# An MLP whose second matmul uses seven products: all units fast, part of their factors made ahead, every sum carried by ScalarE

## The chip, the core and the metric

The kernel runs on one core of one Trainium2 chip. The metric is the device time of one execution in microseconds. The engines are named as in the profile: PE is TensorE, PEld its weight loads, DVE is VectorE, ACT is ScalarE, POOL is GpSimd and SP is SyncE, which here only issues transfers.

## What is computed

A decoder trunk of two layers over 256 positions and a model width of 2048, all in float32. Each layer is a mixer and an MLP with 8192 hidden columns, each followed by a layer norm of the residual.

```python
def sq_relu_mlp(x, w1, w2):
    return jnp.square(jax.nn.relu(x @ w1)) @ w2

def reference(x, ...):
    h = x
    for layer in range(2):
        if layer < 1:
            mix = short_conv_mixer(h, ...)      # (gate_b * conv(gate_c * u)) @ w_out
        else:
            mix = mla_mixer(h, ...)             # latent attention, 16 heads, then @ w_o
        h = layer_norm(ALPHA * h + mix, ln_g[layer, 0], ln_b[layer, 0])
        h = layer_norm(ALPHA * h + sq_relu_mlp(h, mlp_w1[layer], mlp_w2[layer]), ln_g[layer, 1], ln_b[layer, 1])
    return h
```

## The kernel before

**Numbers in two parts.** TensorE takes a rounded form of float32, so every operand is split into a rounded high part and the rest. `split` (L125 to L128) does this for weights: ScalarE casts the high part (L127), VectorE subtracts it to get the low part (L128). A product is then three terms: high by high, high by low, low by high.

**The stream of weights.** All weights pass once, in halves of 128 x 1024 (512 KB), in the order of the list `stream`. SyncE loads a half into one of five raw buffers (`RAW`), ScalarE and VectorE split it into one of eight high and low buffers (`WA`). `take` (L183) hands the next halves to TensorE's code and, first, issues the preparation of halves up to `LOOK` = 5 steps ahead. Each engine works through its instructions in the order in which they were issued, so this look-ahead decides how early a split stands in VectorE's order.

**The stages.** Layer 0's mixer is 48 products of 16 halves' rows each (`opening` for the first four, which are loaded in pieces of growing size, then `lagged`), the convolution, and the product with `w_out`. Layer 1's mixer is the attention and the product with `w_o`. Each MLP works through its hidden columns in eight parts, q = 0 to 7. In each part, eight products (`products`, L288, tile `ps_u`) give 1024 hidden columns, which are squared and split; then the second matmul adds their contribution to the 256 x 2048 result. Parts 0 and 7 do that plainly (`down`). Parts 1 to 6 (`FAST`) are called the fast stages here: they use units of seven products in place of eight (the Strassen-Winograd scheme on 2 x 2 blocks), in `down_pairs` (L634).

**A fast unit.** `prepare` (L141) loads two tiles r1 and r2, which hold the four blocks of the weight, and VectorE builds from them the sums of blocks that the scheme needs: `raw_t` (L162, 128 x 1024, the factors T1 and T3), T2 (L166) and T4 (L169), each 128 x 512. Four splits follow: r1, `raw_t`, r2 and T4 (tile `t`). `fast_products` (L343) then runs seven dots of three matmuls of 512 columns. The factors of the other side, `forms`, come from the hidden columns (`form`, L703).

**Groups and sums.** The 2048 result columns are two groups of 1024; each group has four units per stage. Group 1 is done first (tiles `ps_r`), then group 0 (`ps_f`). Of group 1's four units three are fast and the last is plain, two halves of eight dots (`MIXED = "sssp"`). Seven running sums per group are kept in SBUF, in `acc` and `sums`. At the start of a group ScalarE copies a sum into its PSUM bank (`resumed`, L612) so that the dots add onto it, and at the end copies it out (`put_back`, L616). Three sums of group 0 ("2", "6", "4") start from zero instead, and VectorE adds them (`keep`, L624). There are eight PSUM banks; while the eight products run, four of them (`busy`) take turns for `ps_u`.

Of the kernel before, what the change touches and what calls it, by code (L numbers as in the profile page):

```python
# [37 lines left out]
MIXED = "sssp"  # L38
EVEN = (QC - 1, "22")
# [7 lines left out]
WO_G = 3  # L47
BEHIND = (2, 2, 2, 3, 2, 2, 3)
# [5 lines left out]
def trunk(ctx: ExitStack, tc: tile.TileContext, xT, vecs, lead, w_first, w_in, w_out, w_kv, w_q, w_uk, w_uv,  # L54
# [22 lines left out]

    stream = []
# [4 lines left out]
    def mlp_stream(l):  # L83
        out = []
        for q in range(NQ):
            out += halves(w1[l, q * QC:(q + 1) * QC])
            if q not in FAST:
                out += halves(w2[l, q])
                continue
            for j, kind in enumerate(MIXED):  # L90
                out += [(w2f[l, q, 1, j, 0], w2f[l, q, 1, j, 1])] if kind == "s" else \
                    halves(w2[l, q, 2, j]) + halves(w2[l, q, 3, j])
            out += [(w2f[l, q, 0, j, 0], w2f[l, q, 0, j, 1]) for j in range(QC // 2)]
        return out
# [4 lines left out]
    stream += halves(w_o) + mlp_stream(1)  # L99

# [40 lines left out]
    def prepare(i):  # L141
# [7 lines left out]
        r1, r2 = (load_raw(f"{i}_{j}", src) for j, src in enumerate(stream[i]))  # L149
        out = []  # L150

        def finished(r, name):
# [3 lines left out]

        b22, (b21, b12) = r1[:, BW:], (r2[:, :BW], r2[:, BW:])
# [12 lines left out]
        f = state["fast"].tile([P, 2, BW], F32R, tag="t4", name=f"t4_{i}", bufs=2)  # L170
        split(f[:, 0, :], f[:, 1, :], t4)
        b1, t13, b2 = ([[v.rearrange("p b c -> p (b c)")[:, o:o + BW] for v in w] for o in (0, BW)] for w in out)
        ready[i] = {"11": b1[0], "22": b1[1], "21": b2[0], "T2": b2[1], "T1": t13[0], "T3": t13[1],
                    "T4": [f[:, 0, :], f[:, 1, :]]}
# [8 lines left out]
    def take(halves=2, look=LOOK):  # L183
# [3 lines left out]
        ahead = -sum(size(j) for j in range(i, i + halves))  # L187
        for j in range(i, len(stream)):
            for step in range(size(j)):
                ahead += 1  # L190
                if ahead > look:
                    return [ready.pop(i + k) for k in range(halves)]
# [6 lines left out]
        return [ready.pop(i + k) for k in range(halves)]  # L199
# [143 lines left out]
    def fast_products(ps, x, forms, j, fresh, ready, onto=()):  # L343
# [159 lines left out]
    def summed(ln, pss, add, m0=0):  # L503

        for m, ps in enumerate(pss, m0):
            add(ps, m)
# [40 lines left out]
    ln = Norm(0, ALPHA)  # L547
    for m in range(NC):
# [24 lines left out]
    summed(ln, chain(products(1, z), lagged(NC - 1, z)), residual)  # L573

    def mlp(idx, ln, blocks, fast, begin=None, extra=None, last=False):
# [32 lines left out]
        def resumed(p, g, name, bank):  # L608

            ps = psum(name, bank)  # L610
            if q != FAST[0] or p not in OWN:
# [3 lines left out]
        def put_back(p, g, ps):  # L615
            nc.scalar.copy(place(p, g), ps)  # L616

        def keep(p, g, ps):

            at = place(p, g)  # L620
            if q == FAST[0] and p in OWN:
# [4 lines left out]
        def resume(busy, free, ps, m):  # L626

            b2, b3, b4, b6 = free
            b1, b5, b7, b22 = busy
            for p, bank in {3: (("3", b3),), 4: (("2", b2),), 5: (("4", b4), ("1", b1)), 6: (("6", b6), ("5", b5)),  # L630
                            7: (("7", b7), ("22", b22))}.get(m, ()):
                ps[p] = resumed(p, 1, f"ps_r{p}", bank)

        def down_pairs(h, forms, busy, free, ps):  # L634

            b2, b3, b4, b6 = free
            b1, b5, b7, b22 = busy
            new = set(OWN) if q == FAST[0] else set()
            onto = set(ps) - new
            for j, kind in enumerate(MIXED):  # L640
                if kind == "s":
                    last = j == MIXED.rindex("s")
                    fast_products(ps, h, forms, j, new if j == 0 else (), OWN if last else (), onto)
                    if last:
                        for p in OWN:
                            put_back(p, 1, ps[p])
                        then = {p: resumed(p, 0, f"ps_f{p}", bank) for p, bank in (("3", b1), ("1", b5))}
                    continue
                for two in (((0, "2"), (1, "4")), ((1, "22"), (0, "3"))):
                    w, = take(1, LOOK + 1)  # L650
                    for t, p in two:
                        for kk in range(2):
                            k = 2 * j + kk
                            dot(ps[p], wide_rows(w, kk), held(h[k], t), False, k == QC - 1, (k, p) == EVEN, True)
                    if j == len(MIXED) - 1:
                        if "5" not in then:
                            then.update({p: resumed(p, 0, f"ps_f{p}", bank) for p, bank in (("5", b7), ("7", b6))})
                        for _, p in two:
                            put_back(p, 1, ps[p])
# [528 lines left out]
```

## Time and profile before

| | |
|---|---|
| median of three runs | 2000.02 us |
| lowest and highest run | 1996.99, 2000.58 us |
| span of the profiled execution, first to last instruction | 1994.9 us |
| TensorE clock granted, mean over the span | 1.000 |
| bytes moved, mean rate over the span | 385.85 MB, 193 GB/s |
| VectorE: splits of whole halves (L128, `lo`) | 710 of 1220 ns |
| ScalarE: casts of whole halves (L127, `hi`) | 710 of 1051 ns |

The span is one execution of its own; the runs were timed without the profiler, so the two stand side by side and neither is derived from the other. A row of a group gives the line, the engine, the operation, output and input with their shapes, the count, the busy time, the mean time of one in ns, and the idle time in front of these instructions with what ended most of it. The mean of one instruction contains its latency; instructions of one engine follow each other at a shorter pitch, which the start times in the timeline give.

### The profile page before, as it was taken

How to read it: one execution, taken by the hardware profiler on the slowest of the kernel's cores; microseconds unless marked ns; L12 is line 12 of the kernel's file. 1: busy time of each engine (PE TensorE's matmuls, PEld its weight loads, DVE VectorE, ACT ScalarE, POOL GpSimd, SP SyncE). 2: the span in 40 equal slices, each digit the busy share in tenths (PEclk: the TensorE clock that was granted, in tenths of full speed). 3: DMA queues.
4: the chain of work that ended last, by engine and by line, in shares of the span. 5: the costliest groups of instructions: out<-in, count | busy, mean ns of one | idle time of the engine just before them, and what ended most of it. 6: DMA issues, size and time to landing. Idle time of an engine off the chain costs nothing.

```text
span 1994.9 us, 30180 instructions
## 1 busy us (share of the span) xinstructions
PE 1987.7 (100%) x11110; PEld 1737.2 (87%) x11110; DVE 1709.4 (86%) x2555; ACT 1354.9 (68%) x2154; POOL 2.3 (0%) x21
## 2 busy tenths in 40 slices
PE   9999999999999999999999999999999999999998
PEld 8888888988888888888889998898888888888886
DVE  8667667797999989989978988777899999999985
ACT  6444445586778778777756755558677787887772
POOL 0000000000000000000000000000000000000000
PEclk9999999999999999999999999999999999999999
DMA  8666666565657466574855543656464656656483
GB/s 318 205 191 187 190 190 190 179 193 157 212 170 251 148 216 221 177 243 147 281 171 159 170 140 123 201 180 195 146 233 155 232 161 220 222 178 233 150 269 130
DMA packets 106853, 385.85 MB, mean 193 GB/s; under 512 B 11857, under 2 KB 12625, under 8 KB 106449
## 3 DMA queue, kind: packets, MB, share of 16 engines
q1 hardware_dynamic: 106560, 383.79, 59.5%
q8 instruction: 87, 1.43, 0.3%
q14 instruction: 62, 0.50, 0.1%
q10 hardware_dynamic: 144, 0.13, 0.0%
HBM read 381.78 MB, written 2.10 MB: 192 GB/s over the span
## 4 chain that ended last, share of the span: by engine, by line
PE 98%; DVE 1%; ACT 1%; issue 0%; DVEq 0%; ACTq 0%
PE ps_u L215 20%; PE ps_l L215 13%; PE ps_u L219 10%; PE ps_l L219 7%; PE ps_f L300 4%; PE ps_f L303 4%; PE ps_f L302 4%; PE ps_r L303 4%; PE ps_r L302 4%; PE ps_r L300 4%; PE ps_d L300 2%; PE ps_d L302 2%; PE ps_d L303 2%; PE ps_w L249 2%; PE ps_w L248 2%; PE ps_w L247 2%
## 5 line engine op out<-in xcount | busy, mean ns | idle before, releaser
L128 DVE TENSOR_TENSOR lo<-raw,hi 128x1024 fp32r<-128x1024 f32 x710 | 861.8, 1220 | 190.6 <-ACT hi L127 119.9
L127 ACT CAST hi<-raw 128x1024 fp32r<-128x1024 f32 x710 | 741.8, 1051 | 247.4 <-PE ps_l L215 98.1
L215 PE MATMUL ps_u<-xhl,hi 128*128 128x512 f32 x1792 | 621.7, 392 | 0.0
L219 PE MATMUL ps_u<-xhl,lo 128*128 128x256 f32 x1792 | 498.2, 279 | 0.0
L215 PEld LDWEIGHTS ps_u<-xhl,hi 128*128 128x128 f32 x1792 | 334.5, 187 | 73.6 <-ACT acc L595 0.2
L219 PEld LDWEIGHTS ps_u<-xhl,lo 128*128 128x128 f32 x1792 | 338.1, 189 | 1.8
L215 PE MATMUL ps_l<-xhl_a,hi 128*128 128x512 f32 x704 | 244.1, 393 | 0.0
L219 PE MATMUL ps_l<-xhl_a,lo 128*128 128x256 f32 x704 | 195.4, 279 | 0.0
L215 PEld LDWEIGHTS ps_l<-xhl_a,hi 128*128 128x128 f32 x704 | 132.1, 188 | 29.9
L219 PEld LDWEIGHTS ps_l<-xhl_a,lo 128*128 128x128 f32 x704 | 131.9, 188 | 0.2
L127 ACT CAST hi_t<-raw_t 128x1024 fp32r<-128x1024 f32 x84 | 88.5, 1054 | 45.8 <-DVE raw_t L162 41.4
L162 DVE TENSOR_TENSOR raw_t<-raw,raw 128x1024 f32<-128x1024 f32 x84 | 102.3, 1218 | 1.8 <-DMA raw<-in_w2f_dram 1.5
L128 DVE TENSOR_TENSOR lo_t<-raw_t,hi_t 128x1024 fp32r<-128x1024 f32 x84 | 102.4, 1219 | 0.2
L718 ACT ACTIVATE fp<-fp 128x256 f32<-128x256 f32 x96 | 40.0, 416 | 63.2 <-DVE fp L356 62.6
L215 PE MATMUL ps_l<-z,hi 128*128 128x512 f32 x240 | 82.4, 391 | 0.0
L300 PE MATMUL ps_d<-hi,h 128*128 128x512 f32 x192 | 75.0, 391 | 0.0
L302 PE MATMUL ps_d<-lo,h 128*128 128x512 f32 x192 | 75.0, 390 | 0.0
L303 PE MATMUL ps_d<-hi,h 128*128 128x512 f32 x192 | 74.8, 389 | 0.0
L249 PE MATMUL ps_w<-xd,hi 128*128 128x258 f32 x256 | 72.7, 284 | 0.0
L248 PE MATMUL ps_w<-xd,lo 128*128 128x258 f32 x256 | 72.3, 282 | 0.0
L247 PE MATMUL ps_w<-xd,hi 128*128 128x258 f32 x256 | 72.3, 282 | 0.0
L215 PE MATMUL ps_l<-oT,hi 128*128 128x512 f32 x208 | 71.3, 391 | 0.0
(296 smaller groups left out, 3963.7 us busy)
## 6 DMA issues: line engine op xcount, KB each, us to landing
raw<-in_w_dram SPq DMA_DIRECT2D x344, 512.0 KB, 4.5
raw<-in_w2f_dram SPq DMA_DIRECT2D x168, 512.0 KB, 3.9
raw<-in_w_in_dram SPq DMA_DIRECT2D x88, 512.0 KB, 4.2
raw<-in_w_out_dram SPq DMA_DIRECT2D x32, 512.0 KB, 3.7
raw<-in_w_o_dram SPq DMA_DIRECT2D x32, 512.0 KB, 4.2
raw<-in_w_kv_dram SPq DMA_DIRECT2D x10, 512.0 KB, 3.7
raw<-in_w_q_dram SPq DMA_DIRECT2D x8, 512.0 KB, 4.0
raw<-in_w_uk_dram SPq DMA_DIRECT2D x8, 512.0 KB, 3.9
```

Of the source, the lines that this page charges most:

```text
L127: nc.scalar.copy(hi, src)
L128: nc.vector.tensor_tensor(lo, src, hi.bitcast(F32), ALU.subtract)
L162: nc.vector.tensor_tensor(t.rearrange(two, a=2), b12.unsqueeze(1).to_broadcast([P, 2, BW]), r1.rearrange(two, a=2), ALU.subtract)
L215: nc.tensor.matmul(ps, w[blk // 8][0][:, blk % 8, :], x, start=first, stop=False)
L219: nc.tensor.matmul(ps[:, :T], w[blk // 8][1][:, blk % 8, :], x[:, :T], start=False, stop=last)
L247: nc.tensor.matmul(ps[:, :W], hi, x[k][:, :W], start=k == 0, stop=False)
L248: nc.tensor.matmul(ps[:, :W], lo, x[k][:, :W], start=False, stop=False)
L249: nc.tensor.matmul(ps[:, :W], hi, x[k][:, W:], start=False, stop=k == NC - 1)
L300: nc.tensor.matmul(ps, x[0], w[0], start=first, stop=False, skip_group_check=onto)
L302: nc.tensor.matmul(ps[:, at], x[0], w[1][:, at], start=False, stop=False, skip_group_check=onto)
L303: nc.tensor.matmul(ps, x[1], w[0], start=False, stop=last, skip_group_check=onto)
L718: nc.scalar.activation(f, f, AF.Relu)
```

## The change

- All eight units of a fast stage are fast. The groups alternate: the first stage does group 1 and then 0, the next 0 and then 1, and so on. The second group's sums "3", "1", "5" and "7" stay in PSUM into the next stage, where the same group goes first.
- Every sum is put back by ScalarE and copied in by ScalarE (`FRESH` is empty, so `keep` always copies and `begun_sum` copies in except at the first stage). At the last unit of a group each sum is put back right after its last dot, and the next group's sum is copied into the bank that was freed.
- For eighteen units (`EARLY`: in each of the six fast stages two units of MLP 0 and one of MLP 1) the factors are made ahead by `making`: GpSimd's queue loads the two tiles, VectorE runs the same three operations, GpSimd's queue stores T1 and T3 as one tile and T2 and T4 as another into DRAM. Such a unit later loads three tiles of 512 KB and one of 256 KB, and has four splits and no sums to build. The making has buffers of its own, two of each kind for MLP 0 and one for MLP 1. The program places it from the seventh chunk of the first mixer on and in the attention; the built order has parts of it earlier.
- `spent` issues steps of the look-ahead in mid-product too: in `products` after half of it, and in `fast_products` after the dots "1" and "7", there up to two steps further ahead.
- The transposes of the residual at the end of layer 1's stages take the blocks in another order.

In the built order, TensorE has 10947 matmuls in place of 10995, VectorE loses 34 additions (L624) and gains the making's 54 operations, GpSimd's queue has 36 loads and 36 stores, and SyncE issues 778 transfers in place of 742.

```diff
-MIXED = "sssp"
-EVEN = (QC - 1, "22")
+EARLY = {0: ((1, 0), (1, 2)), 1: ((1, 1),)}
+FRESH = ()
...
+MAKE_FROM = 6
...
+    def groups(q):
+        return (1, 0) if (q - FAST[0]) % 2 == 0 else (0, 1)
...
+            for i, g in enumerate(groups(q)):
+                for j in range(QC // 2):
+                    out.append((w2f[l, q, g, j, 0], w2f[l, q, g, j, 1]) + made.get((l, q, i, j), ()))
...
+    def making(l, pool):
+        for (k, q, i, j), (to13, to24) in made.items():
...
+            for r, src in zip((r1, r2), w2f[l, q, groups(q)[i], j]):
+                nc.gpsimd.dma_start(r, src)
+            yield
...
+            nc.vector.tensor_tensor(t.rearrange(two, a=2), b12.unsqueeze(1).to_broadcast([P, 2, BW]),
+                                    r1.rearrange(two, a=2), ALU.subtract)
+            nc.vector.tensor_tensor(r1[:, :BW], b22, t[:, :BW], ALU.subtract)
+            nc.vector.tensor_tensor(r1[:, BW:], b21, r1[:, :BW], ALU.subtract)
+            nc.gpsimd.dma_start(to13, t)
+            nc.gpsimd.dma_start(to24, r1)
...
+        if len(stream[i]) == 4:
+            r1, t13 = load_raw(f"{i}_0", stream[i][0]), load_raw(f"{i}_1", stream[i][2])
+            finished(r1, f"{i}_1")
+            yield
+            t24 = load_raw(f"{i}_2", stream[i][3])
+            b21 = raws.tile([P, 1024], F32, tag="raw", name=f"raw{i}_3")[:, :BW]
+            nc.sync.dma_start(b21, stream[i][1][:, :BW])
+            finished(t13, f"{i}_t")
+            yield
+            finished(t24, f"{i}_2")
...
-            mm_run([(w, ps)], x, 0, NC, NC, turned=None if i else turned)
+            mm_run([(w, ps)], x, 0, NC // 2, NC, turned=None if i else turned)
+            spent(1)
+            mm_run([(w, ps)], x, NC // 2, NC, NC)
...
             dot(ps[p], b[r], a[l], p in fresh, p in ready, onto=p in onto)
+            if p in "17":
+                spent("17".index(p) + 1)
+            if then:
+                then(p)
...
+        def keep(p, g, ps, since):
             at = place(p, g)
-            if q == FAST[0] and p in OWN:
+            if p not in FRESH or (since == FAST[0] and p in OWN):
                 nc.scalar.copy(at, ps)
             else:
                 nc.vector.tensor_tensor(at, at, ps, ALU.add)
...
+            def turn(p):
+                keep(p, first, ps[p], max(q - 1, FAST[0]) if p in order[:4] else q)
+                i = order.index(p) + 1
+                if i < len(order):
+                    begin_next(order[i], banks[p])
...
+                fast_products(ps, h, forms, j, new - held_on if j == 0 else (), ps if j == n - 1 else (),
+                              set(ps) - (new - held_on), turn if j == n - 1 else None)
+            for j in range(n):
+                fast_products(after, h, forms, j, new if j == 0 else (), after if j == n - 1 else (),
+                              set(order) - new, end if j == n - 1 else None)
...
+        if m >= MAKE_FROM:
+            next(before_mlp, None)
```

More of the change, by code (lines that the diff above doesn't have):

```diff
@@ L169, in prepare @@
         nc.vector.tensor_tensor(t4, b21, b12, ALU.subtract)
[L170 to L174, printed above, removed]
+        ready[i] = {**named((("11", "22"), ("T1", "T3"), ("21", "T2"))), "T4": fourth(t4)}
         yield
@@ L186, in take, with spent @@
         state["next"] += halves
-        ahead = -sum(size(j) for j in range(i, i + halves))
+        state["taken"] = i, sum(size(j) for j in range(i, i + halves))
+        spent(0, look)
+        return [ready.pop(i + k) for k in range(halves)]
+    def spent(n, look=LOOK):
+        i, total = state["taken"]
+        ahead = -total
         for j in range(i, len(stream)):
@@ L190, in take @@
                 ahead += 1
-                if ahead > look:
-                    return [ready.pop(i + k) for k in range(halves)]
+                if ahead > look + n:
+                    return
                 if j < 2 * HEAD:
@@ L624, in keep @@
                 nc.vector.tensor_tensor(at, at, ps, ALU.add)
[L626 to L659, printed above, removed]
-            n = QC // 2
-            onto = set(then) - new
-            then.update({p: psum(f"ps_f{p}", bank) for p, bank in (("2", b2), ("6", b4), ("4", b22))})
-            for j in range(n):
-                fast_products(then, h, forms, j, set(then) - onto if j == 0 else (), then if j == n - 1 else (), onto)
-            for p, _, _ in FACTORS:
-                (put_back if p in onto or p in new else keep)(p, 0, then[p])
-            return (b3, b1, b5, b7), (b6, b2, b4, b22)
@@ L684, in last_sum @@
             nc.scalar.copy(finals[n, t], block(n, t))
-        busy, free = (0, 1, 2, 3), (4, 5, 6, 7)
+        busy, sums_in, places = (0, 1, 2, 3), {}, {"3": 4, "1": 5, "5": 6, "7": 7}
         for q in range(NQ):
@@ L773, in mlp @@
             else:
-                busy, free = down_pairs(h, forms, busy, free, begun)
+                busy, sums_in, places = down_pairs(h, forms, sums_in, places, busy[3])
     def to_wide(block, put, h):
```

86 lines of the change are left out of this document (67 added, 19 removed).

## The prediction

> **What bounds the kernel now.** I read the first lines of the page, then its chain of waits, then the table of stretches for single stages, then the groups and the timeline around each stage's end.
>
> ```profile
> span 1994.9 us, 30180 instructions
> PE 1987.7 (100%) x11110; PEld 1737.2 (87%) x11110; DVE 1709.4 (86%) x2555; ACT 1354.9 (68%) x2154; POOL 2.3 (0%) x21
> ...
> PE 98%; DVE 1%; ACT 1%; issue 0%; DVEq 0%; ACTq 0%
> ```
>
> TensorE is busy for all but 7.2 us of the span and makes 98% of the chain. So a matmul removed is worth its pitch, if what feeds TensorE keeps up. VectorE, at 86% over the span, is the engine to look at next. In stretches (columns: us; busy time and count of PE, PE's weight loads, DVE, ACT, POOL; granted clock; DMA share; GB/s) one stage of the MLP with a fast second matmul, the last such stage of MLP 0, and the two halves of a stage's second matmul (group 1, then group 0) read:
>
> ```profile
> 536.00:619.23 83.23, 83.23 (x429) 71.28 (x428) 78.12 (x101) 66.47 (x104) 0.00 (x0) 1.00 0.60 199
> 868.91:953.06 84.15, 83.69 (x429) 71.12 (x428) 78.52 (x102) 66.34 (x103) 0.00 (x0) 1.00 0.59 198
> 746.85:766.64 19.79, 19.79 (x90) 16.39 (x89) 19.69 (x25) 16.16 (x25) 0.00 (x0) 1.00 0.57 188
> 766.64:785.68 19.04, 19.04 (x85) 15.77 (x84) 18.97 (x21) 15.07 (x23) 0.00 (x0) 1.00 0.56 174
> ```
>
> The clock is granted in full. In the second matmul VectorE is busy for 19.69 of 19.79 us and for 18.97 of 19.04: there it has no time left. Whether TensorE waits is decided by how long before its use the last split of a stage is done, which the timeline tells for the best and the worst stage of MLP 0, and for one of each kind in MLP 1 (start, length):
>
> ```profile
> 696.01 1.22 DVE L128 TENSOR_TENSOR lo_t<-raw_t,hi_t 128x1024 fp32r<-128x1024 f32 x1
> 699.28 0.39 PE L302 MATMUL ps_f<-lo_t,forms 128*128 128x512 f32 x1
> ...
> 948.19 1.22 DVE L128 TENSOR_TENSOR lo_t<-raw_t,hi_t 128x1024 fp32r<-128x1024 f32 x1
> 949.89 0.39 PE L302 MATMUL ps_f<-lo_t,forms 128*128 128x512 f32 x1
> ...
> 1472.24 1.22 DVE L128 TENSOR_TENSOR lo_t<-raw_t,hi_t 128x1024 fp32r<-128x1024 f32 x1
> 1475.48 0.39 PE L302 MATMUL ps_f<-lo_t,forms 128*128 128x512 f32 x1
> ...
> 1892.32 1.22 DVE L128 TENSOR_TENSOR lo_t<-raw_t,hi_t 128x1024 fp32r<-128x1024 f32 x1
> 1894.21 0.39 PE L302 MATMUL ps_f<-lo_t,forms 128*128 128x512 f32 x1
> ```
>
> The margins are 2.05, 0.48, 2.02 and 0.67 us (use, less start, less 1.22). Read so, the twelve fast stages have 1.76, 0.93, 2.05, 0.67, 1.20, 0.48 in MLP 0 and 2.02, 1.68, 1.23, 0.91, 1.51, 0.67 in MLP 1. TensorE is full, and VectorE is nowhere more than 2.1 us behind being the bound.
>
> **What it removes from TensorE.** Each fast stage of before has one plain unit of two weight halves among seven fast units: 24 matmuls of 512 columns and two halved ones more, 88 in group 1 where group 0 has 84. The rows of the two halves give 19.79 - 19.04 = 0.75 us. All eight units become fast, so 12 x 0.75 = **-9.0 us**. The pitch per matmul (19.04 / 84 = 0.227) makes it 3 x 0.227 = 0.68 a stage, 8.2; I take the direct difference.
>
> **What it does to VectorE in the fast stages.**
>
> ```profile
> 780.62 1.22 DVE L128 TENSOR_TENSOR lo_t<-raw_t,hi_t 128x1024 fp32r<-128x1024 f32 x1
> 781.75 1.22 DVE L128 TENSOR_TENSOR lo<-raw,hi 128x1024 fp32r<-128x1024 f32 x1
> 782.89 0.69 DVE L128 TENSOR_TENSOR t<-raw,t 128x512 fp32r<-128x512 f32 x1
> 783.49 1.22 DVE L128 TENSOR_TENSOR lo<-raw,hi 128x1024 fp32r<-128x1024 f32 x1
> ...
> L162 DVE TENSOR_TENSOR raw_t<-raw,raw 128x1024 f32<-128x1024 f32 x84 | 102.3, 1218 | 1.8 <-DMA raw<-in_w2f_dram 1.5 <-DVE lo L128 0.3
> L169 DVE TENSOR_TENSOR raw<-raw 128x512 f32<-128x512 f32 x84 | 57.8, 688 | 1.3
> L166 DVE TENSOR_TENSOR raw<-raw,raw_t 128x512 f32<-128x512 f32 x84 | 57.7, 687 | 1.2
> L624 DVE TENSOR_TENSOR acc<-acc,ps_f 128x512 f32<-128x512 f32 x24 | 16.3, 680 | 0.1
> ```
>
> Back to back, a row of 1024 starts 1.14 us after the one before it (780.62 to 781.75, 781.75 to 782.89) and one of 512 takes 0.60. A plain unit costs VectorE two splits, 2.28. A fast unit costs raw_t, three splits of 1024 and three operations of 512: 4 x 1.14 + 3 x 0.60 = 6.36. A unit whose factors were made ahead keeps four splits: 3 x 1.14 + 0.60 = 4.02, 2.34 less. Per stage, then: plain to fast -4.08; made units +2.34 each (two in MLP 0, one in MLP 1); TensorE arriving earlier -0.75. The 34 adds into sums that go to ScalarE are 34 x 0.60 / 12 = 1.7 a stage. They lie ahead of places where VectorE idles anyway:
>
> ```profile
> 724.74 1.23 DVE L128 TENSOR_TENSOR lo<-raw,hi 128x1024 fp32r<-128x1024 f32 x1 [1.43 <-ACT hi L127]
> ...
> 730.19 1.22 DVE L128 TENSOR_TENSOR lo<-raw,hi 128x1024 fp32r<-128x1024 f32 x1 [0.82 <-ACT hi L127]
> ```
>
> By itself that time would only lengthen these 1.43 and 0.82 us. The change also issues one step of the look-ahead sooner, in mid-product, so I count the 1.7 as carried to the stage's end (ends 0, where the eight hi and lo buffers are already full, and 1.7).
>
> A made unit adds a wait. Its third load (t24) takes the raw buffer that the unit before it gives back at lo_t. From there VectorE has about 4.02 us of splits ahead of the new one; the load and ScalarE's cast must fit into them:
>
> ```profile
> L127 ACT CAST hi<-raw 128x1024 fp32r<-128x1024 f32 x710 | 741.8, 1051 | 247.4 <-PE ps_l L215 98.1 <-DMA raw<-in_w_dram 29.9 <-PE ps_d L303 27.9
> ...
> raw<-in_w_dram SPq DMA_DIRECT2D x344, 512.0 KB, 4.5
> raw<-in_w2f_dram SPq DMA_DIRECT2D x168, 512.0 KB, 3.9
> out_dram<-acc SPq DMA_DIRECT2D x8, 256.0 KB, 2.4
> ```
>
> 3.9 to 4.5 + 1.05 - 4.02 = 0.93 to 1.53; I take 1.25. Behind the waiting split stand, on VectorE, all later splits and the evacuations of the next stage, and TensorE waits for those. The margin so moves by -4.08 + 4.68 - 2.50 + 1.70 - 0.75 = -0.95 in MLP 0 and -4.08 + 2.34 - 1.25 + 1.70 - 0.75 = -2.04 in MLP 1. Where that is more than a stage has, TensorE waits for the rest: 0.02 + 0.28 + 0.47 = 0.8 in MLP 0, 0.02 + 0.36 + 0.81 + 1.13 + 0.53 + 1.37 = 4.2 in MLP 1, **+5.0** together. Ends: 0, if the splits keep up; 8.7 with the wait at 1.53; 18.1 if besides only half of the 1.7 is carried.
>
> **ScalarE.** It has 66.47 of 83.23 us of work in a stage, and its copies into and out of PSUM fall by 36, against 24 more casts: 0. What hides it is ScalarE's 17 us of idle time a stage; at the turn from group to group a late copy costs TensorE the pause that one stage of before shows, which I leave as it is (ends -0.9 and 0, the 84.15 against 83.23 above):
>
> ```profile
> 937.97 0.50 PE L300 MATMUL ps_f<-t,h 128*128 128x512 f32 x1 [0.46 <-ACT acc L616]
> ```
>
> **The making of factors, opening.** Eighteen units' factors are made: two loads on GpSimd's queue, three VectorE operations (2.34), two stores on that queue. In the built order, four of the loads (2.10 MB) are issued at the very start, and the first operation of making stands as VectorE's eighth, behind the first piece's splits and ahead of the second piece's. It waits for two loads, 1.05 MB. Behind it stand all splits of the opening, and TensorE needs these at once.
>
> ```profile
> 4.00:8.00 4.00, 4.00 (x28) 3.82 (x28) 3.41 (x15) 3.52 (x15) 0.00 (x0) 1.00 0.96 320
> 8.00:12.00 4.00, 4.00 (x24) 3.46 (x23) 3.37 (x11) 3.46 (x11) 0.00 (x0) 1.00 0.99 374
> 12.00:16.00 4.00, 4.00 (x24) 3.47 (x24) 3.40 (x7) 2.47 (x7) 0.00 (x0) 1.00 1.02 427
> 16.00:20.00 4.00, 4.00 (x21) 3.26 (x21) 3.36 (x5) 3.29 (x6) 0.00 (x0) 1.00 1.03 413
> 20.00:24.00 4.00, 4.00 (x27) 3.63 (x26) 3.11 (x6) 3.10 (x6) 0.00 (x0) 1.00 1.02 407
> ...
> 15.96 2.18 ACT L127 CAST hi<-first 128x512 fp32r<-128x512 f32 x4 [1.45 <-DMA first<-in_w_first_dram]
> ```
>
> The DMA engines are full here and ScalarE waits for them, so 2.10 MB more push the opening back by 2.10 / 0.413 = **+5.1 us**. Ends: 3.3, where only the 1.05 MB ahead of VectorE's wait count (1.05 / 0.320), and 8, where both delays add. The Trainium skill ("DMA: Bandwidth & Descriptors", Specifications) puts the limit of a core on HBM at about 358 GB/s; the rows show 427, so the measurement decides. By the page this term would be an estimated 5.9.
>
> **The making of factors, later.** Makings 3 to 12 stand in VectorE's order between some 33 split steps of the mixer:
>
> ```profile
> first<-in_w_first_dram SPq DMA_DIRECT2D x2, 1024.0 KB, 11.2
> ...
> 50.00:100.00 50.00, 50.00 (x290) 43.86 (x289) 32.23 (x47) 22.55 (x31) 0.30 (x3) 1.00 0.68 206
> ...
> 985.00:1065.00 80.00, 79.97 (x462) 70.25 (x461) 61.25 (x107) 43.49 (x75) 0.53 (x1) 1.00 0.55 173
> ```
>
> The 290 matmuls are 18 weight halves of 16, so a half feeds TensorE for 50.00 / 18 = 2.78 us, and the ten makings lie 33 x 2.78 / 10 = 9.2 us apart; 2.10 MB and 9.2 x 206 GB/s = 1.90 MB make 4.0 MB per making, 435 GB/s against the 407 to 427 seen. VectorE has the 2.34 free (32.23 of 50), but it waits in order for each load, and a reload for the store two makings earlier. I take **+4.0**. Ends: 0, where the look-ahead of five halves, 14 us, covers the lateness, and 19, if each making takes 12.5 us (11.2 for its megabyte to land, as in the opening, and the 1.14 before the next one's turn), 10 x 3.3 less 14. MLP 1's six makings stand where VectorE has 19 of 80 us free: 0; without that cover, 6 x 2.34 = 14.
>
> **The sum.** Span 1994.9 - 9.0 + 5.1 + 4.0 + 5.0 = 2000.0. The median of the runs, 2000.02, lies 5.1 above the span, so the forecast is **2005.1 us**, 0.25% slower. Its own range is 2001 (makings hidden) to 2012 (opening 8, stage ends 8.7).
>
> **The rivals.** *The DMA engines carry the second queue at little cost (faster).* If a 512 KB load lands in 3.0 us (the 2.4 of 256 KB and 0.26 / 0.413 more), the wait of a made unit is 0.03; MLP 0 then gains margin and MLP 1 loses 0.82, which costs 0.15. With the opening at 3.3, makings at 0 and the pause of 0.9 gone: 1994.9 - 9.0 + 3.3 + 0.2 - 0.9 + 5.1 = 1993.6. It holds from a load time of about 3.5 down. For it: VectorE and the look-ahead have room in the mixer. Against: loads in company take 3.9 to 4.5.
>
> *The splits keep up, the makings don't vanish (no change).* Stage ends 0, the rest as forecast: 2000.1. For it: the look-ahead is deeper and the adds are gone. Against: 18.97 of 19.04.
>
> *The lateness isn't recovered (slower still).* The wait at 1.53, half of the 1.7 carried, stage ends 18.1: 2018.2. For it: the eight buffers limit how far ahead VectorE can get. A slow GpSimd queue leads to the same region, with makings at 19: 2020.1. The Trainium skill ("SBUF — State Buffer", SBUF: two separate sides) warns that transfers issued by GpSimd wait for descriptors while VectorE runs an operation on two ports. No run here shows such a transfer yet.
>
> That the saving on TensorE doesn't come is no rival: the built order has 48 matmuls fewer.
>
> **How the numbers follow.** Forecast 0.36, faster rival 0.26, no change 0.21, slower still 0.17. What a measurement here can tell from no change is about 0.2%, 4 us. Faster: the first rival and a little of the second's spread, 0.27. Same: the rest of the second and the lower end of the forecast's range, 0.23. Slower: 0.50. The range of 1990 to 2021 takes in the rivals' times with some spread, and leaves out cases such as makings at 19 together with stage ends at 18.
>
> **What would show it.** A fast stage of 82.5 us where TensorE doesn't wait and both halves of its second matmul equally long, 19.04: the 9.0. In the opening, VectorE's eighth operation idle behind the GpSimd loads, and the fifth and sixth chunks' products 5 us later than before. Between 30 and 130 us, pauses of TensorE of 4 us in sum. At the ends of MLP 1's stages, TensorE idle with VectorE's split as the releaser, about 0.7 a stage, and none in most of MLP 0's. I am wrong if VectorE is done 2 us ahead at the stage ends, if the opening ends when it did, or if TensorE waits for ScalarE's copies at the turn of the groups.

## The result, and the profile after

| | before | after |
|---|---|---|
| median of the runs | 1999.59 us (4 runs) | 2068.86 us (4 runs, 2066.88 to 2071.84) |
| ratio, 95% interval | | 1.0348 [1.0334, 1.0363] |
| span of the profiled execution | 1994.9 us | 2067.5 us |

The forecast was 2005.1 with a range to 2021. The sign was right; the size was out by more than a factor of ten. Of the four executions of the kernel `nomake` further down, one took 6497.85 us against 2031.29 to 2032.71 for the others, and its ratio rests on these three. The head of the page after, with its chain of waits:

```profile
span 2067.5 us, 30316 instructions
PE 2017.7 (98%) x11062; PEld 1731.3 (84%) x11062; DVE 1735.0 (84%) x2581; ACT 1356.1 (66%) x2142; POOL 41.1 (2%) x93
...
PE 55%; DVE 23%; DMA 11%; issue 7%; ACT 4%; POOL 0%; DVEq 0%; SPq 0%; ACTq 0%; POOLq 0%
```

TensorE's share of the chain fell from 98% to 55%, and transfers are in it with 11% where they had none. Yet VectorE's and ScalarE's busy shares are lower than before: they don't have too much work, they wait. Cut at the starts of the matmuls, the two traces compare like this (us):

| stretch | before | after | difference | forecast |
|---|---|---|---|---|
| to the end of the first four products | 27.88 | 34.33 | +6.4 | +5.1 |
| rest of the first mixer's products | 245.17 | 267.04 | +21.9 | +4.0 |
| w_out and the first plain part of MLP 0 | 179.72 | 179.76 | 0 | 0 |
| six fast stages of MLP 0 | 500.3 | 517.8 | +17.5 | -3.7 |
| last plain part of MLP 0 and its norm | 145.14 | 154.06 | +8.9 | 0 |
| attention, w_o, first plain part of MLP 1 | 296.20 | 296.20 | 0 | 0 |
| six fast stages of MLP 1 | 503.0 | 519.9 | +16.9 | -0.3 |
| rest | 92.81 | 93.48 | +0.7 | 0 |

(The forecast's -9.0 and +5.0 are divided over the two MLPs: -4.5 + 0.8 and -4.5 + 4.2.) Two groups of stretches carry all but 0.7 us of it: 37.2 us where factors are made, and 34.4 in the fast stages. For the first, here are the timeline of VectorE in the opening (start, length, idle before and what ended it) and sums of waits (total, times, longest): of VectorE in the rest of the mixer and at the end of MLP 0, and of TensorE in the opening, in the same rest of the mixer and at the end of MLP 0:

```profile
5.03 0.89 DVE L157 TENSOR_TENSOR lo<-lead,hi 128x128 fp32r<-128x128 f32 x4
10.01 1.22 DVE L123 TENSOR_TENSOR m<-m,m 128x1024 f32<-128x1024 f32 x1 [4.09 <-DMA m<-in_w2f_dram]
11.15 0.42 DVE L598 TENSOR_TENSOR xhl_a<-lead,xhl_a 128x256 fp32r<-128x256 f32 x1
```

```profile
DVE m L123 <- DMA m<-in_w2f_dram: 26.4, 6, 6.6
...
DVE m L123 <- DMA m<-in_w2f_dram: 8.9, 3, 5.5
...
PE ps_g L268 <- DVE xhl_a L598: 4.9, 1, 4.9
...
PE ps_l L272 <- DVE lo L157: 13.6, 8, 4.3
...
PE ps_d L355 <- DVE fh L415: 3.9, 1, 3.9
```

In the opening the second piece's split (11.15) stands behind the making (10.01), which waits 4.09 us for its loads. Later the same wait comes every 10 us or so. In stretches (columns as in the prediction) here are the rest of the mixer before, then after, with two parts of it and the end of MLP 0's last part, and then a fast stage after in three: the first group's four units, the second's, and the next products:

```profile
27.88:273.06 245.18, 245.18 (x1413) 215.08 (x1412) 167.97 (x248) 115.30 (x155) 1.39 (x14) 1.00 0.66 202
```

```profile
34.33:301.37 267.04, 253.44 (x1413) 219.92 (x1412) 190.88 (x281) 115.70 (x158) 21.82 (x52) 0.97 0.80 267
...
50.00:100.00 50.00, 50.00 (x290) 43.84 (x288) 35.46 (x52) 20.17 (x27) 7.85 (x17) 1.00 0.91 326
100.00:150.00 50.00, 38.84 (x194) 31.81 (x192) 31.53 (x46) 14.31 (x20) 10.39 (x21) 0.93 0.95 337
...
1044.21:1096.96 52.75, 48.88 (x218) 40.14 (x217) 43.66 (x69) 27.07 (x42) 4.86 (x9) 0.94 0.72 247
...
612.79:631.84 19.05, 19.05 (x86) 15.77 (x85) 17.56 (x23) 13.83 (x21) 0.00 (x0) 1.00 0.57 183
631.84:653.77 21.93, 20.46 (x85) 15.18 (x84) 18.29 (x19) 17.91 (x26) 0.00 (x0) 1.00 0.58 194
653.77:699.09 45.32, 45.32 (x257) 39.16 (x256) 41.15 (x58) 34.70 (x55) 0.00 (x0) 1.00 0.71 236
```

A wait costs TensorE more than its own length. In the rest of the mixer its waits sum to 13.6 us. The other 8.3 of the 21.9 are work that took longer: the same 1413 matmuls kept it busy for 253.44 us in place of 245.18. The granted clock is 0.97 there where it was 1.00, and it falls where TensorE waits: it is 1.00 between 50 and 100 us, without a wait, and 0.93 between 100 and 150, where TensorE is idle for 11.2 of the 13.6 us. It is the same in the opening (0.94, one wait of 4.9) and at the end of MLP 0 (0.94, one of 3.9). Before had no such waits, and its clock was 1.00 throughout. That the waits lower the clock is read from their places; it was not tested by itself. In the fast stages after it is 1.00, so the second group has none of this.

The first group of units takes 19.05, as forecast from the 84 matmuls (19.04). The second group of units takes 21.93 with VectorE busy for only 18.29 of it, and the products 45.32 where they took 44.39. The timeline of ScalarE in that stage shows the unit made ahead and, after it, the turn from group to group:

```profile
627.47 1.05 ACT L156 CAST hi<-raw 128x1024 fp32r<-128x1024 f32 x1 [1.30 <-DMA raw<-made]
629.61 0.62 ACT L156 CAST t<-raw 128x512 fp32r<-128x512 f32 x1 [1.09 <-DMA raw<-in_w2f_dram]
630.14 0.58 ACT L696 COPY acc<-ps_f 128x512 f32<-128x512 f32 x1
630.62 0.59 ACT L696 COPY sums<-ps_f 128x512 f32<-128x512 f32 x1
631.10 0.60 ACT L689 COPY ps_f<-sums 128x512 f32<-128x512 f32 x1
631.61 1.06 ACT L156 CAST hi<-raw 128x1024 fp32r<-128x1024 f32 x1
632.56 0.60 ACT L689 COPY ps_f<-sums 128x512 f32<-128x512 f32 x1
633.08 1.08 ACT L696 COPY sums<-ps_f 128x512 f32<-128x512 f32 x2
634.04 0.62 ACT L689 COPY ps_f<-sums 128x512 f32<-128x512 f32 x1
```

And on TensorE, the dot that the last of these copies releases, and on VectorE the split behind the cast of 631.61:

```profile
634.71 0.50 PE L355 MATMUL ps_f<-hi_t,forms 128*128 128x512 f32 x1 [0.54 <-ACT ps_f L689]
...
632.70 1.23 DVE L157 TENSOR_TENSOR lo<-raw,hi 128x1024 fp32r<-128x1024 f32 x1 [1.75 <-ACT hi L156]
```

A made unit makes ScalarE wait twice (1.30 and 1.09 us). Then the copies out and in stand in a row with the casts, ScalarE has no gap, TensorE waits for a copied sum and VectorE for a cast.

### The profile page after: what moved, and what is told of

Read it like the earlier page. It is cut to its first block, busy times and chain, and to the rows that moved or that the text cites. A ratio compares the mean times of both kernels' runs of the same rounds, so it can differ in the third digit from the quotient of the medians.

```text
span 2067.5 us, 30316 instructions
## 1 busy us (share of the span) xinstructions
PE 2017.7 (98%) x11062; PEld 1731.3 (84%) x11062; DVE 1735.0 (84%) x2581; ACT 1356.1 (66%) x2142; POOL 41.1 (2%) x93
## 3 DMA queue, kind: packets, MB, share of 16 engines
q8 instruction: 87, 1.43, 0.3%
## 4 chain that ended last, share of the span: by engine, by line
PE 55%; DVE 23%; DMA 11%; issue 7%; ACT 4%; POOL 0%; DVEq 0%; SPq 0%; ACTq 0%; POOLq 0%
PE ps_u L268 10%; PE ps_l L268 10%; DVE lo L157 6%; DMA raw<-in_w2f_dram 5%; PE ps_u L272 5%; PE ps_l L272 5%; DVE lo_t L157 3%; DVE raw_t L213 3%; DMA m<-in_w2f_dram 2%; ACT hi L156 2%; PE ps_d L355 2%; PE ps_d L358 2%; PE ps_d L357 2%; DMA raw<-in_w_dram 2%; DVE raw L217 2%
## 5 line engine op out<-in xcount | busy, mean ns | idle before, releaser
L268 PE MATMUL ps_u<-xhl,hi 128*128 128x512 f32 x1792 | 628.9, 396 | 0.0
L268 PE MATMUL ps_l<-xhl_a,hi 128*128 128x512 f32 x704 | 250.2, 400 | 0.0
L272 PE MATMUL ps_l<-xhl_a,lo 128*128 128x256 f32 x704 | 199.2, 285 | 13.6 <-DVE lo L157 13.6
L156 ACT CAST hi_t<-raw_t 128x1024 fp32r<-128x1024 f32 x78 | 82.1, 1053 | 84.0 <-DVE raw_t L213 64.0
L213 DVE TENSOR_TENSOR raw_t<-raw,raw 128x1024 f32<-128x1024 f32 x78 | 95.0, 1217 | 4.4 <-DMA raw<-in_w2f_dram 4.3
L157 DVE TENSOR_TENSOR lo_t<-raw_t,hi_t 128x1024 fp32r<-128x1024 f32 x78 | 95.0, 1218 | 3.1 <-ACT hi_t L156 2.5
L355 PE MATMUL ps_f<-hi_t,forms 128*128 128x512 f32 x176 | 69.3, 405 | 11.0 <-ACT ps_f L689 8.4
L156 ACT CAST t<-raw 128x512 fp32r<-128x512 f32 x96 | 59.4, 619 | 21.4 <-DMA raw<-in_w2f_dram 14.3
```

The lines of the kernel that those rows point to most:

```text
L156: nc.scalar.copy(hi, src)
L157: nc.vector.tensor_tensor(lo, src, hi.bitcast(F32), ALU.subtract)
L213: nc.vector.tensor_tensor(t.rearrange(two, a=2), b12.unsqueeze(1).to_broadcast([P, 2, BW]), r1.rearrange(two, a=2), ALU.subtract)
L268: nc.tensor.matmul(ps, w[blk // 8][0][:, blk % 8, :], x, start=first, stop=False)
L272: nc.tensor.matmul(ps[:, :T], w[blk // 8][1][:, blk % 8, :], x[:, :T], start=False, stop=last)
L355: nc.tensor.matmul(ps, x[0], w[0], start=first, stop=False, skip_group_check=onto)
```

## The experiments

Times are medians where several runs were made and single runs else; 'lateness' is how much longer than 21 x 0.2267 us a unit's matmuls took, by their starts. In all kernels the four units ahead of the turn are on time within 0.06 us, but for the odd stage; so the table gives the fifth to eighth, as medians over the second to sixth fast stage of MLP 0 and of MLP 1, and the time. Stages are read from one profiled execution each; that of `fresh` was 6.4 us faster than its median, that of `gate2` 3.8. Differences of 2 or 3 us between the times mean little: before itself took 1997.5 to 2001.3 beside these kernels. `no_copy_in` and the `g2_` kernels leave a part of the work out, so they no longer compute the reference's sums.

| kernel | MLP 0: units 5, 6, 7, 8 | MLP 1: units 5, 6, 7, 8 | time, us |
|---|---|---|---|
| after | 1.00, 0.61, 0, 1.17 | 2.06, 0.68, 0, 0.55 | 2068.9 |
| nomake | 1.54, 0.33, 0, 1.05 | 1.43, 0.30, 0, 1.09 | 2032.4 |
| fresh | 1.08, 0, 0, 1.57 | 1.52, 0.49, 0, 1.69 | 2069.2 |
| no_copy_in | 0, 0.03, 1.01, 2.07 | 0, 0, 0.73, 2.07 | 2033.9 |
| all_added | 4.45, 0.06, 0.03, 2.00 | 4.46, 0.93, 0, 2.01 | 2070.7 |
| no_spent | 0.68, 0.65, 1.11, 2.03 | 0.68, 0.64, 1.11, 2.03 | 2050.0 |
| gate2 | 1.77, 0.61, 0, 0.73 | 2.18, 0.68, 0, 0.56 | 2045.1 |
| g2_no_copy_in | 0, 0, 0.02, 2.67 | 0.17, 0.73, 0.11, 1.54 | 2042.9 |
| g2_no_copies | 0, 0, 0, 2.90 | 0, 0, 1.13, 1.35 | 2040.0 |
| g2_three | 0.23, 0.73, 0, 0.19 | 1.22, 0.88, 0, 0.36 | 2035.3 |
| g2_three_no_copies | 0, 0, 0, 1.31 | 0, 0, 0.67, 1.35 | 2030.3 |

**Making left out.**

```diff
-EARLY = {0: ((1, 0), (1, 2)), 1: ((1, 1),)}
+EARLY = {}
```

> The changed kernel without any factors made ahead (EARLY empty): all units build their factors in place. Opening, mixer and the end of MLP 0 go back to before's lengths by both theories, -37.3 us. Theory V (VectorE bounds the fast stages): 18 made units' relief of 2.34 us is lost, the fast stages get up to 42 us longer, so the sum is about 2060 to 2074. Theory S (ScalarE's copies at the turn from group to group bound them): the relief hardly counted, and the time is about 2032 to 2042.

Measured: 2032.38 us, ratio 1.0170 [1.0150, 1.0191]. The mixer is back at 245.17, the end of MLP 0 at 145.82. The six fast stages take 517.9 and 518.5 us, as with making (517.8 and 519.9). So making costs 36.5 us and gains nothing in the fast stages. That fits theory S, but not it alone: a stage of this kernel (first group, second group, next products) reads

```profile
757.63:776.70 19.07, 19.07 (x87) 15.77 (x85) 18.97 (x26) 13.10 (x19) 0.00 (x0) 1.00 0.42 136
776.70:799.09 22.39, 21.34 (x87) 15.05 (x85) 22.18 (x25) 18.59 (x28) 0.00 (x0) 1.00 0.49 164
799.09:844.17 45.08, 45.08 (x257) 39.11 (x256) 41.11 (x57) 34.72 (x55) 0.00 (x0) 1.00 0.72 237
```

VectorE is busy for 22.18 of 22.39 us of the second group here, against 18.29 of 21.93 with made units. The same length has another limit.

**Three sums added by VectorE.**

```diff
-FRESH = ()
+FRESH = ("2", "6", "4")
```

> The changed kernel with the sums of 2, 6 and 4 started from zero and added by VectorE (FRESH has these three). Theory S (ScalarE's copies, 0.59 out and 0.58 in for each sum, seven sums within the 4.8 us of one unit, bound the turn): the 11.4 us that TensorE waited for copies into PSUM (ps_f, L689) go, and with them part of the slower pitch after a stall: 2050 to 2058 us. Theory V (VectorE bounds the fast stages): 60 to 70 additions of 0.60 us come back onto it, 2075 to 2100 us.

Measured: 2069.2 us, ratio 1.0351 [1.0332, 1.0370], the same as after. Neither theory's number came. In MLP 0 the lateness is nearly the same in sum; the six stages there are 4.8 us shorter, 3.6 of it because the products run at their faster pitch (last section) and 1.2 in the first stage. MLP 1 is 1.4 longer. So where the three sums are added doesn't decide. With the loads of the makings held back as well (the next edit), the time was 2088.27 us, ratio 1.0453 [1.0438, 1.0469]: 4.8 less than with that edit alone, where 2014 to 2024 had been expected if both edits gained.

**Making later in time.**

```diff
             for r, src in zip((r1, r2), w2f[l, q, groups(q)[i], j]):
+                nc.gpsimd.tensor_copy(r[:, :2], state["gate"][:, :2].bitcast(F32))
                 nc.gpsimd.dma_start(r, src)
```

`state["gate"]` is the chunk of z, of the attention's output or of the residual that was last computed when the making is reached. In `summed` the residual's addition is moved ahead of the making for this.

> The changed kernel, but each making's loads are held back until a chunk of the mixer's output (or of the attention's, for MLP 1) exists, one making per 16.6 us of TensorE's time, by a copy of two columns on GpSimd ahead of each load. Theory A (VectorE waits in its order for GpSimd's loads and all splits wait behind it): the 37.3 us by which the opening (+6.5), the rest of the first mixer (+21.9) and the end of MLP 0 (+8.9) are longer go away, all but some 4: 2032 to 2036 us, fast stages as in the changed kernel (81 to 82 us of products and second matmul where it had 85 to 87, no: unchanged at 85 to 87). Theory B (the additional bytes themselves cost the time, wherever they are moved): the same bytes are moved, so it stays within 10 us of 2069.

Measured: 2093.06 us, ratio 1.0465 [1.0440, 1.0490], 24 us slower than after. The opening is back at 28.07 us, but the rest of the mixer is at 268.74, w_out and the next part at 202.60 (+22.9, with one wait of TensorE of 19.3 for `z`, whose last steps stand behind a making in VectorE's order), the attention at 309.89 (+13.7). Theory A's number was wrong, its mechanism wasn't: VectorE's waits and two of its rows read

```profile
DVE m L124 <- DMA m<-in_w2f_dram: 81.6, 11, 8.6
...
159.01 1.23 DVE L124 TENSOR_TENSOR m<-m,m 128x1024 f32<-128x1024 f32 x1 [8.32 <-DMA m<-in_w2f_dram]
181.31 1.23 DVE L124 TENSOR_TENSOR m<-m,m 128x1024 f32<-128x1024 f32 x1 [6.08 <-DMA m<-in_w2f_dram]
```

Each making now waits 7.4 us (81.6 / 11). Holding the loads back had moved the operations with them, close behind their loads in VectorE's order.

**With the operations held back too.**

```diff
             yield
+            nc.gpsimd.tensor_copy(t[:, :2], state["gate"][:, :2].bitcast(F32))
             b22, (b21, b12) = r1[:, BW:], (r2[:, :BW], r2[:, BW:])
```

> The kernel with the loads held back, and the making's three VectorE operations held back as well, by one more chunk (16.6 us of TensorE's time in the first mixer), through a copy of two columns on GpSimd into the tile that they write. Theory A (the cost of a making is VectorE's wait for its loads, because its operations stand directly behind them in the order): the loads have landed (7.3 us) when VectorE comes to them, and the first mixer, w_out and the attention go back to 245, 180 and 296 us: 2093 - 60 = 2033 us, within 6. Theory B (bytes on the DMA engines, or the pace of GpSimd's queue): the same transfers are made at the same rate, so more than 2070 us.

Measured: 2045.09 us, ratio 1.0234 [1.0217, 1.0251]: 12 above theory A's 2033, and 25 below what theory B gave as its least. The rest of the mixer, and 50 us of it in which the makings are dense:

```profile
28.46:273.63 245.17, 245.17 (x1412) 215.06 (x1411) 185.89 (x272) 114.66 (x155) 35.48 (x74) 1.00 0.79 270
150.00:200.00 50.00, 50.00 (x289) 43.87 (x288) 43.41 (x70) 22.97 (x31) 12.66 (x24) 1.00 0.86 307
```

TensorE never waits: 245.17 us at 270 GB/s (307 in the 50 us), where after took 267.04 at 267. So neither the bytes in themselves nor VectorE's work are the cost; its waits are. 48 us lie between gate and gate2. What is left of the making is mainly in the attention, 306.03 against 296.20. There VectorE still waits five times for the makings' loads, 16.2 us together, and TensorE waits twice, 2.3 and 3.2 us. With nomake at 2032.4, making still isn't worth its price.

**What bounds the fast stages.** No sum copied into PSUM; in the second kernel every sum that doesn't stay is added by VectorE; in the third the steps of the look-ahead in mid-product are left out. All three are without making.

```diff
 no_copy_in:
-            return p in FRESH or (q == FAST[0] and p in OWN)
+            return True
 all_added:
-FRESH = ()
+FRESH = ("3", "1", "5", "7", "2", "6", "4")
 no_spent:
+        if n:
+            return
         i, total = state["taken"]
```

> The kernel without making, and without any copy of a running sum into PSUM, so that the earlier stages' sums are left out; the copies out stay. ScalarE has 7 copies of 0.58 less at each turn and 3 less among the products. Theory S (ScalarE is late at the turn): the first unit behind the turn, 1.3 to 2.5 us late, is on time or within 0.3, and the last unit is less late than 1.1: a fast stage falls from 86.3 to 83 to 84, the time from 2032 to 1995 to 2010 us. Theory V (VectorE's splits bound the stage): the late units stay, 2025 to 2032 us.

> The kernel without making, with every sum that doesn't stay in PSUM started from zero and added by VectorE: ScalarE has no copy at the turns, VectorE 7 additions of 0.60 more at each. Theory S: the first unit behind the turn is on time; the last unit is later, since VectorE gets 8 us more in a stage of 86: about 2050 to 2100 us in sum, with the lateness moved from the fifth unit to the eighth. Theory V: the fifth unit is later too, by the 4 us of additions ahead of its splits.

> The kernel without making and without the steps of the look-ahead issued in mid-product. If the deeper look-ahead is what keeps the units before the turn on time (the prediction counted 1.7 us a stage as carried by it), the fast stages get 1 to 3 us longer each, 2045 to 2070 us. If it does nothing, 2032.

Measured: 2033.91, 2070.66 and 2050.01 us. Without copies in, the fifth unit is on time and the eighth is late by 2.07 in place of 1.05: the lateness moved and the sum stayed, as neither pure theory had it. So ScalarE's copies aren't the only limit: without them VectorE's splits are late at the stage's end, and a stage still takes 86 us. The same stage of this kernel, second group only:

```profile
777.25:799.45 22.20, 20.66 (x87) 15.30 (x85) 22.00 (x25) 15.44 (x22) 0.00 (x0) 1.00 0.50 165
```

ScalarE fell from 18.59 to 15.44 us, VectorE stayed full. With all sums added by VectorE the fifth unit is late by 4.45 (from the third fast stage on; in the second by 0.04), the price of seven additions ahead of its splits (7 x 0.60 = 4.2): theory V's reading. Without `spent` the lateness in sum is 5.09 where it was 3.02 (means over the same stages of MLP 0): the deeper look-ahead is worth 2.1 us a stage, near the 1.7 that the prediction counted as carried.

**The made units' own loads.** These kernels start from gate2. They leave out the copies in; the copies out as well between the first and last fast stage; the fourth load; and the last two together.

```diff
 g2_no_copies:
+                if q in (FAST[0], FAST[-1]):
-                nc.scalar.copy(at, ps)
+                    nc.scalar.copy(at, ps)
 g2_three:
-            b21 = raws.tile([P, 1024], F32, tag="raw", name=f"raw{i}_3")[:, :BW]
-            nc.sync.dma_start(b21, stream[i][1][:, :BW])
+            b21 = t24[:, :BW]
```

> The kernel whose makings don't hold VectorE up (gate2), with no running sum copied into PSUM, so that earlier stages' sums are left out. Here VectorE has 77.1 us of work in 87 of a stage of MLP 0, some 4 less than without making. Theory S+V (two limits lie close together, ScalarE at the turn and VectorE's splits; either alone holds the stage at 86): with VectorE relieved by the made units AND the copies gone, the fifth unit's 1 to 2 us go and the eighth's don't grow to 2.1 in MLP 0 as they did without making: a stage of MLP 0 falls to 83.5 to 84.5. Theory M (the made unit's own loads hold the splits up): the stall stays, moved to the seventh and eighth unit, 86.

> As the last, and the copies out are left out too but in the first and the last fast stage, so that the sums are wrong. In the stages between, ScalarE has no copy at the turn at all. Theory S+V: a stage of MLP 0 at 83 to 84, of MLP 1 (one made unit) 84 to 85. Theory M: no better than with the copies out, 85 to 86.

> gate2 with three loads in a made unit in place of four: the block 21 isn't loaded, and T2's columns stand in for it, so that product 2 is wrong there. ScalarE's wait for that block (1.09 us per made unit in MLP 0) and one raw buffer are saved. Theory M (a made unit gives its relief of 2.34 back by its loads' waits, 1.30 and 1.09): the last unit is on time in MLP 0 and a stage is 1 to 2 us shorter, 84 to 85 in MLP 0. Theory S: the turn's lateness stays, at most 0.5 us shorter.

> Both: no copies of sums between the first and the last fast stage, and made units of three loads. By all theories together nothing is left that holds a stage of MLP 0 up: 82.5 to 83.4 us there (38.1 for the second matmul, 44.4 to 45.3 for the products). If it stays above 84, a cause is not yet known.

Measured: 2042.88, 2039.95, 2035.32 and 2030.32 us. Without copies in, a stage of MLP 0 takes 86.6 in the mean, as theory M had it. Without any copy the eighth unit is still late by 2.90 in MLP 0, although VectorE has less work there than without making: theory M again. With three loads instead of four, a stage of MLP 0 gives (second group, first g2_three, then g2_three_no_copies)

```profile
774.09:793.96 19.87, 19.56 (x86) 15.46 (x84) 17.21 (x19) 16.86 (x25) 0.00 (x0) 1.00 0.58 181
```

```profile
769.53:789.20 19.67, 19.34 (x85) 15.69 (x84) 18.27 (x20) 11.47 (x13) 0.00 (x0) 1.00 0.61 195
789.20:833.59 44.39, 44.39 (x257) 39.12 (x256) 36.48 (x50) 29.96 (x46) 0.00 (x0) 1.00 0.68 224
```

19.87 in place of 21.93. The six stages of MLP 0 fall from 516.1 to 509.5 us, and the eighth unit's lateness from 0.73 to 0.19. The fifth's falls from 1.77 to 0.23 although all copies are there, which theory S didn't have; two of the five stages still have 1.27 and 4.83. In MLP 1, with one made unit a stage, they fall by 3.5 only. With the copies gone as well, this stage is at 83.14 us in all (19.08, 19.67, 44.39), near the 82.5 of the expectation; the six together take 507.5, since one stage takes 88.90, and MLP 1's are at 85.8 in the mean. In that one stage TensorE waits for splits and casts for 3.4 us, and the granted clock in its second matmul is 0.96, against 1.00 in the stage above. What made the splits late there is not known.

**VectorE made late in the kernel before.** In the second fast stage of MLP 0, five or nine additions that change nothing.

```diff
+                if idx == 1 and q == 2:
+                    late = raws.tile([P, 1024], F32, tag="raw", name="late")
+                    nc.vector.memset(late, 0.0)
+                    for _ in range(5):
+                        nc.vector.tensor_tensor(late, late, late, ALU.add)
                 busy, free = down_pairs(h, forms, busy, free, begun)
```

> The kernel before with five additions of 128x1024 and one fill of the same size more on VectorE, in the second matmul of the second fast stage of MLP 0, which change nothing in the output. VectorE gets 5 x 1.14 us and the fill, some 6.5 us. By the prediction's ledger that stage has 0.93 us of margin, so TensorE waits 5 to 6 us in it, the next stages are as before (the look-ahead is refilled within the products). Theory P (the slower pitch of the products, 0.236 us per matmul of 512 columns where before has 0.230, is a state that a wait of TensorE leaves behind): at least one of the later stages' products, none of which waits, takes 45.1 to 45.3 us in place of 44.39. Theory Q (the pitch comes from the changed code of the products): all stay at 44.39.

> The same with nine additions: four more, 4.6 us more of VectorE, so TensorE waits 4.6 us longer than with five, if VectorE's work is paid one for one there. Theories P and Q as with five.

Measured: 2008.05 and 2013.71 us. That stage takes 92.75 and 99.98 us in place of 83.23. The four additions more, 4.6 us of VectorE, cost 7.2. The second matmul of that stage, with five and with nine, reads

```profile
581.10:629.45 48.35, 43.29 (x174) 32.45 (x173) 47.43 (x55) 35.10 (x53) 0.00 (x0) 0.96 0.51 161
```

```profile
580.76:636.35 55.59, 46.08 (x175) 34.51 (x173) 51.85 (x59) 34.77 (x52) 0.00 (x0) 0.91 0.42 141
```

TensorE is idle for 5.06 and 9.51 us: 4.45 more, one for one. The other 2.8 are the same matmuls, busy for longer at a granted clock of 0.91 in place of 0.96. The next stage is at 83.23 in both, so a stage starts afresh, as the ledger had it. On the pitch of the products theory P doesn't stand: all later stages of MLP 0 have it as before. Nor does Q: in b_late5 the first fast stage of MLP 1, with before's code and no wait near it, has the slower one (85.06 against 84.25).

## Why the prediction was wrong

**Matmuls, -9.0: right.** Four fast units take 19.05, and both groups have 84 matmuls. But the saving exists only where nothing else is late.

**Opening, +5.1: right in mechanism, near in size.** +6.4 measured; the making's first operation stood where the built order had it, waited 4.09 us, and all splits stood behind it. TensorE waited 4.9 for one of them, and was busy for longer at a clock of 0.94. The loads of 1 MB landed after 15.7 us in place of 11.2, as the bytes would have it. With the loads held back (gate) the opening is 28.07; no run parts the bytes from the wait here.

**Makings 3 to 12, +4.0 with ends 0 and 19: mechanism named, term mis-sized.** 21.9 was measured, beyond the upper end (which is 17 and not 19: 11.2 and 1.14 make 12.3). TensorE's waits, 13.6, lie within the ends; the 8.3 of longer work had no term. The step that failed for the waits is "the look-ahead of five halves, 14 us, covers the lateness". It covers it once. VectorE waited 26.4 us in this stretch for the loads of six makings; between two of them, some 10 us apart, it has about 35% free (32.23 of 50 busy, before), from which the making's own 2.34 must come too: an estimated 10 x 0.35 - 2.34 = 1.2 us of recovery against 4.4 of wait. The price of the transfers was worked out from their bytes and a rate, and gate2 shows that the rate was no limit. What counts is how long a load takes to land, since VectorE's operation stands right behind it. For the time of the makings, 34 to 165 us, the transfers' table of after has

```profile
raw<-in_w_in_dram SPq DMA_DIRECT2D x41, 512.0 KB, 6.0
made<-m POOLq DMA_DIRECT2D x21, 512.0 KB, 6.3
m<-in_w2f_dram POOLq DMA_DIRECT2D x18, 512.0 KB, 7.4
```

That is 7.4 us on GpSimd's queue, and 6.0 for the same size on SyncE's beside it, where before had 4.3 in the same stretch: both queues are slow in company. The Trainium skill ("DMA: Bandwidth & Descriptors", Anatomy of one DMA — SWDGE (gpsimd) path) fits a fixed 2.0 us and 436 GB/s to such a transfer, an estimated 3.2 us; the rows here show more than twice that, and they decide.

**MLP 1's makings, 0: wrong.** +8.9 at the end of MLP 0, where VectorE waits for the making's loads three times, 8.9 us together. That the two numbers are equal is chance: of the +8.9, TensorE was idle for 5.0, 3.9 of it in one wait, and 3.9 more were longer work (149.07 us busy in place of 145.12). The prediction looked for VectorE's free time there (19 of 80 us) and priced the work; it didn't price the wait, which it had priced in the mixer.

**Fast stages, -9.0 + 5.0: wrong, +34.4 measured.** By the starts of the matmuls: -9.0 for the matmuls, +39.1 of lateness in the twelve second matmuls (0.9 before), +5.3 of slower products. Two steps failed. "ScalarE ... 0. What hides it is ScalarE's 17 us of idle time a stage": the mean over a stage hides that the copies now all fall into the one unit at the turn, 14 copies of some 0.5 us each, 7 us, into 4.8 us of TensorE's time. The fifth unit's 1.0 to 2.1 us vanish without the copies in, so the copies take part in them; they don't make them alone, since with all copies but three loads (g2_three) the median is 0.23 in MLP 0. The prediction named it at its end as what would make it wrong, and gave it no chance. And "I take 1.25" for a made unit's wait: the stage shown has 1.30 for the third load, as taken, and 1.09 more for the fourth, which the ledger left out. The two together, 2.39 us of waiting by ScalarE, are as long as the relief of 2.34. That made units gained nothing in the fast stages is what nomake shows.

**The ledger of VectorE: nearly right.** Without made units it gives -4.08 + 1.70 - 0.75 = -3.1 a stage, less a margin of 1.2 in the mean: 1.9 late. no_copy_in, where VectorE is left as the limit, has 3.3 in the mean of MLP 0's later stages. The granted clock was 1.00 in these stages, so it doesn't explain the difference, which stays open.

**The rivals.** The slower rival (2018.2) had the right direction for the stage ends. None had the turn, and the sums were made of limits taken one by one, each of the others taken as met; that several lie so close that a stage stays near 86 us when one is gone came out only by removing them in turn. **The term between span and run**, 5.1, was too large as well: it sets the median beside the span of another execution. After's median lies 1.4 above its span, and each of after's four executions 1.7 to 1.9 above its own.

No version here beats the kernel before. The nearest of those that leave nothing out is nomake, at 2032.4.

## What to carry to other kernels

A load that an in-order engine waits for costs that engine the load's latency and everything queued behind it, wherever there is spare time; put the using instruction a full latency later in its order (48 us between gate and gate2), and don't count a look-ahead as cover more than once. Price a wait of TensorE above its length: here waits of 13.6 us cost 21.9, at a granted clock of 0.97. Copies that an average hides must be priced against the one unit into which they fall. When a stage is near several limits, taking one away only moves the lateness: take them away singly and together before you trust any one cause.

## Not expected

The eight products, the same 256 matmuls with no wait in them, took 44.39 us in some stages and 45.1 to 45.3 in others, at a granted clock of 1.00 in both. The matmuls of 512 columns follow each other at 0.236 us in place of 0.230; those of 256 stay at 0.117. In before all fast stages have the faster pitch; in the changed kernel those of MLP 0 from the third on, and some of MLP 1, have the slower one. It comes and goes with stages, not inside them as a rule. Neither a wait of TensorE shortly ahead nor the changed code explains it (b_late5, b_late9), and its cause stays open.
